# Fewer divided matrix products, at other places, in a tuned hybrid-attention layer; three small steps of the order moved

## The chip, the cores and the metric

One core of a Trainium2 chip runs the whole layer. The metric is device time in microseconds (us) of one execution, the median over runs. Each engine of the core (TensorE = PE, VectorE = DVE, ScalarE = ACT, GpSimd = POOL, SyncE = SP) works through its own list of instructions in order; they meet at semaphores.

## The reference, cut to what matters

```python
h = x                                              # 256 tokens x 2048
n = rmsnorm(h, g_mix);  z = n @ w_in               # 2048 x 5120
q, k, v, u = split(z)
a = moba_attention(q, k, v, bias)                  # 8 heads of 128; one block of 256 keys, so causal
c = conformer_conv(u)                              # gate, 31 taps per channel, layernorm, silu
h = h + concat(a, c) @ w_out                       # 2048 x 2048
h = h + cross_attention(rmsnorm(h), rmsnorm(mem))  # 4 heads, 256 memory tokens; wq, wk, wv, wo
h = h + square(relu(rmsnorm(h) @ w1)) @ w2         # 2048 x 8192 x 2048
return rmsnorm(h, g_final)
```

All in float32. About 200 MB of weights are read once.

## The kernel before, in words

The weights are cut into 200 chunks of 128 x 2048 numbers, one for each **step** of the program: 0 to 15 the conv projection (U), 16 to 23 V, 24 to 39 Q and K, 40 to 47 keys and values of the memory, 48 to 63 w_out, 64 to 67 wq, 68 to 71 wo, and from 72 four times 16 steps of w1 and 16 of w2 (w1 at 72, 104, 136 and 168).

Float32 accuracy comes from three products of rounded parts: a chunk is loaded (`raw`), ACT rounds it (`wh`), DVE takes the rest (`wl`, in six of the early steps POOL does), and the activations are split in the same way. `weight_stationary` (U, QK, w_out, wq, w1) issues, for each of 16 pairs of a 128-row piece i and a 128-column piece m of the chunk, `wh` x high, `wh` x low, `wl` x high, each over 256 tokens: 48 **products** in a step, numbered 0 to 47, and four units of 12. `act_stationary` (V, memory values, w2) keeps the activations still and moves 512 columns; there are 24 of these in a step.

The table `PARTED` (L43) names products which are **divided**: L342 to L344 issue the product as one matmul over 64 tokens and one over 192, with the weights loaded for both. Before, 8 steps had three divided products each.

The order is written by hand. The loop at L1007 goes through the steps and calls hooks: "early", "pre" and "late" ahead of a step's products, "mid" ahead of a unit (the number behind it), "post" behind the last. Within it ACT splits the chunk two steps ahead (`split_high`), DVE or POOL too (`split_low`), and `fill` puts as many of the 248 convolution taps between as DVE should have room for, by a cost model.

- `WARM` (L45): so many transposes of constants run on PE ahead of the first product.
- `spread_m` (L449 to L451): two transposes spread the memory's rmsnorm factor `r_m` over 128 partitions, ahead of unit 2 of step 16. `r_m` comes from `st_m.chain` (ahead of unit 2 of step 15), seven small DVE instructions and an ACT square root.
- `self_attention(b)` (L481), for two heads each, b = 0 to 3, s0 = 28 + 4b: `scores` behind step s0, softmax in s0 + 1, `transposes` of the probabilities ahead of unit 2 of s0 + 2 (then two ACT copies), `values` ahead of unit 2 of s0 + 3, `evac_o` at the start of s0 + 4. All of them take turns on two PSUM banks called `sm`.
- Cross attention, head h: `cx_q` (a DVE copy of the query), `cx_s` (scores on PE, maximum on DVE, exponentials on ACT, scaling on DVE), `cx_t` (transposes on PE, a copy on ACT), `cx_v` (values on PE). In step 66, ahead of unit 2, stood `cx_t(0)` and then `cx_s(1)`; `cx_v(0)` stands behind the step. At that step's start `wo_split0` (L747) splits a chunk of wo, two instructions on ACT and two on DVE.

Of the kernel before, what the change touches and what calls it, by code (L numbers as in the profile page):

```python
# [30 lines left out]
U0, V0, QK0, MK0, MV0, WOUT0, WQ0, WO0, MLP0, NSTEP = 0, 16, 24, 40, 44, 48, 64, 68, 72, 200  # L31
# [7 lines left out]
WOUT_ORDER = [(0, 0), (1, 0), (2, 0), (0, 1), (1, 1), (2, 1), (3, 0), (3, 1)]  # L39
STEP_US = 5.25  # L40


PARTED = {2: (3, 7, 11), 6: (24, 28, 32), 24: (3, 7, 11), 50: (3, 7, 11), 77: (24, 28, 32),  # L43
          104: (3, 7, 11), 136: (3, 7, 11), 168: (3, 7, 11)}
WARM = 14  # L45

ROOM = 128
ACT_SHIFT = (0, 0, 96, 96)
# [34 lines left out]
def tile_hybrid_block(ctx: ExitStack, tc: tile.TileContext, xT, memT, w, par, rel, gfin, out):  # L83
# [12 lines left out]
    def ring(shape=(P, 512)):  # L96
        return sb.tile(list(shape), F32, tag="ring", name=nm("ring"), bufs=7)

    def small():
        return sb.tile([P, 16], F32, tag="small", name=nm("small"), bufs=4)  # L100

    def bank(tag):
        return Bank(ps.tile([P, 512], F32, tag=tag, name=nm(tag), bufs={"mm": 4, "cv": 2, "sm": 2}[tag]))

    def mm(bk, o, lhsT, rhs, stop):
        pe.matmul(o, lhsT=lhsT, rhs=rhs, start=not bk.begun, stop=stop, skip_group_check=True)  # L106
        bk.begun = True
# [40 lines left out]
    warm = bank("sm")  # L148
    for i in range(WARM):
        pe.transpose(warm.ap[:, (i % 4) * P:(i % 4 + 1) * P], ones, ident)  # L150
# [4 lines left out]
    def at(place, j, fn, frac=0):  # L155
        hooks.setdefault((place, j), []).append((frac, fn))
# [97 lines left out]
    def spread(r):  # L254
        bk = bank("sm")
        for t in range(2):
            pe.transpose(bk.ap[:, t * P:(t + 1) * P], r[:, t:t + 1].to_broadcast([P, P]), ident)
        rb = sb.tile([P, T], F32, tag="Rb", name=nm("Rb"), bufs=2)
        act.copy(rb, bk.ap[:, :T])
        return rb  # L260
# [4 lines left out]
    def pair(ap):  # L265
        return ap.rearrange("p (a b) -> p a b", a=2)
# [33 lines left out]
    def weight_stationary(j, banks, kg, acts, kts=4, cols=512, last=None):  # L300
        units = []
        nf = cols // P
        for i in range(kts):
            def unit(i=i):
                for m in range(nf):
# [5 lines left out]
                    for n, (a, b) in enumerate(((h, hi), (h, lo), (l, hi))):  # L311
                        stop = last and i == kts - 1 and n == 2
                        if 3 * (nf * i + m) + n in PARTED.get(j, ()):
                            mm(bk, o[:, 0:64], a, b[:, 0:64], False)
# [19 lines left out]
    def block(j0, n, kind, acts, evac, place="pre", lag=0, tag="mm"):  # L334
        banks = []

        def open_banks():
            banks.extend([bank(tag), bank(tag)])

        for k in range(n):  # L340
            def make(k=k):
                if k == 0:  # L342
                    open_banks()
                return kind(j0 + k, banks, k, acts, last=(k == n - 1))  # L344
            pe_units[j0 + k] = make
        at(place, j0 + n + lag, lambda: evac(banks))
# [101 lines left out]

    def spread_m():  # L449
        RB["m"] = spread(r_m)  # L450
    at("mid", 16, spread_m, 2)  # L451
    for g in range(4):
        at("pre", (38, 39, 40, 42)[g], lambda g=g: split_act_group(g, memraw[g], G_MEM))

# [15 lines left out]
    def mix_tiles(key):  # L470
        if key not in mix:
            mix[key] = shifted(f"mix{key}", (S_SHIFT[key] + MIX_STEP) % ROOM)
        return mix[key]

    def evac_split(dst, i, src):
        hi, lo = dst
        act.activation(hi[:, i, :], src, AF.Copy)
        dve.tensor_sub(lo[:, i, :], src, hi.bitcast(F32)[:, i, :])

    def self_attention(b):  # L480
        st = {}  # L481
        s0 = QK0 + 4 * b + 4
        heads = (2 * b, 2 * b + 1)

        def evac_qk(banks):
            for h, bk in zip(heads, banks):
                st["qk", h] = ring((P, 2, T))
                dve.tensor_tensor(st["qk", h], pair(bk.ap), RB["qk"], op=OP.mult)

        def scores():  # L490
            for h in heads:
                bk = bank("sm")
                q, k = st["qk", h][:, 0, :], st["qk", h][:, 1, :]
                mm(bk, bk.ap[:, 0:P], q[:, 0:P], k[:, 0:P], True)
                mm(bk, bk.ap[:, P:3 * P], q[:, P:T], k, True)
                st["s", h] = bk.ap

        def softmax_a():
            for h in heads:
                pr, s = ring(), small()  # L500
                st["p", h], st["z", h] = pr, s
                for t, (lo, hi), bs in ((0, (0, P), bias[:, h, P:T]), (1, (P, 3 * P), bias[:, h, :])):
                    dve.tensor_tensor_reduce(pr[:, lo:hi], in0=st["s", h][:, lo:hi], in1=bs, scale=1.0,
                                             scalar=MASK, op0=OP.add, op1=OP.max, accum_out=s[:, t:t + 1])
                dve.tensor_scalar(s[:, 2:4], s[:, 0:2], -1.0, None, op0=OP.mult)

        def softmax_b():
            for h in heads:
                pr, s = st["p", h], st["z", h]
                for t, (lo, hi) in ((0, (0, P)), (1, (P, 3 * P))):  # L510
                    act.activation(pr[:, lo:hi], pr[:, lo:hi], AF.Exp, bias=s[:, 2 + t:3 + t],
                                   accum_out=s[:, 4 + t:5 + t])

        def softmax_c():
            for h in heads:
                pr, s = st["p", h], st["z", h]
                dve.reciprocal(s[:, 6:8], s[:, 4:6])
                for t, (lo, hi) in ((0, (0, P)), (1, (P, 3 * P))):
                    act.activation(pr[:, lo:hi], pr[:, lo:hi], AF.Copy, scale=s[:, 6 + t:7 + t])

        def transposes():
            for h in heads:
                bk = bank("sm")
                for i in range(3):
                    pe.transpose(bk.ap[:, i * P:(i + 1) * P], st["p", h][:, i * P:(i + 1) * P], ident)  # L525
                st["t", h] = ring()
                act.copy(st["t", h][:, 0:3 * P], bk.ap[:, 0:3 * P])

        def values():
            for h in heads:  # L530
                bk = bank("sm")
                c = slice(h * P, (h + 1) * P)
                mm(bk, bk.ap[:, 0:T], vv[0][:, 0, c], st["t", h][:, 0:T], False)
                mm(bk, bk.ap[:, P:T], vv[0][:, 1, c], st["t", h][:, T:3 * P], True)
                st["o", h] = bk.ap[:, 0:T]

        def evac_o():
            for h in heads:
                evac_split(mix_tiles(MIX[h // 4]), h % 4, st["o", h])

        block(QK0 + 4 * b, 4, weight_stationary, act_pair, evac_qk, place="early")
        at("post", s0, scores)
        at("pre", s0 + 1, softmax_a)
        at("late", s0 + 1, softmax_b)
        at("late", s0 + 1, softmax_c)
        at("mid", s0 + 2, transposes, 2)
        at("mid", s0 + 3, values, 2)
        at("pre", s0 + 4, evac_o)

    for b in range(4):  # L550
# [124 lines left out]
    def wq_units(h):  # L675
        def make():
            bk = cx["bank", h] = bank("cv")
            o = bk.ap[:, 0:T]
            j = WQ0 + h

            def unit(g):
                def go():
                    for i in range(4):
                        kt = 4 * g + i
                        s = slice(kt * P, (kt + 1) * P)
                        mm3(bk, o, (wh[j][:, s], wl[j][:, s]), act_pair(kt), kt == KT - 1)
                return go
            return [unit(g) for g in range(4)]
        return make

    def cx_q(h):
        cx["q", h] = ring()
        dve.tensor_copy(cx["q", h][:, 0:T], cx["bank", h].ap[:, 0:T])
# [17 lines left out]
    def cx_t(h):  # L711
        bk = bank("sm")
        for m in range(2):
            for t in range(2):
                pe.transpose(bk.ap[:, m * T + t * P:m * T + (t + 1) * P], cx["p", h][:, t, m * P:(m + 1) * P], ident)  # L715
        cx["t", h] = ring((P, 2, T))
        act.copy(cx["t", h], pair(bk.ap))

    def cx_v(h):
        bk = bank("sm")  # L720
        for m in range(2):
            mm(bk, bk.ap[:, 0:T], kv[1][:, m, h * P:(h + 1) * P], cx["t", h][:, m, :], m == 1)
        cx["o", h] = bk.ap[:, 0:T]

    def cx_e(h):
        if not cx_o:
            mix.clear()
            cx_o.append(mix_tiles("a0"))
        evac_split(cx_o[0], h, cx["o", h])

    for h in range(N_CROSS):
        pe_units[WQ0 + h] = wq_units(h)
        at("early", WQ0 + h + 1, lambda h=h: cx_q(h))
        if h < 3:
            at("mid", WQ0 + h + 1, lambda h=h: cx_s(h), 3 if h == 0 else 2)
        if h < 2:
            at("mid", WQ0 + h + 2, lambda h=h: cx_t(h), 2)
            at("post", WQ0 + h + 2, lambda h=h: cx_v(h))
            at("early", WQ0 + h + 3, lambda h=h: cx_e(h))

# [338 lines left out]
```

## Time and profile before

| | us |
|---|---|
| three runs, median (lowest to highest) | 1159.45 (1157.51 to 1162.56) |
| the profiled execution, its own time | 1160.12 |
| its span, first to last instruction | 1158.3 |
| PE busy | 1144.4 of the span |
| DVE, ACT, POOL busy | 705.5, 540.3, 123.2 |

PE's matmuls are pipelined: a busy PE is not one at its peak. How fast it goes is read from how many matmuls start in a stretch, or from the distance of their starts. The granted TensorE clock was 0.997 of full speed over the span.

### The profile page before, as it was taken

To read this page: it belongs to the slowest core of one execution; us is meant where nothing else is said; L and a number is where in the kernel's file an instruction comes from. 1 tells how busy PE (TensorE), PEld (TensorE's weight loads), DVE (VectorE), ACT (ScalarE), POOL (GpSimd) and SP (SyncE) were. 2 spreads that over 40 slices of the span, in tenths; PEclk is the share of its full clock that TensorE was granted. 3 is DMA by queue.
4 is the path that set the end of the run, shared out by engine and by line. 5 is a ranking of instruction groups with operands and counts; after the bars stand their busy time and mean duration, and the time that the engine had idled before them with its cause. 6 is when DMAs were issued, how large, how long until landed. Compare 5 with 4: busy or idle time off the path is not lost.

```text
span 1158.3 us, 18581 instructions
## 1 busy us (share of the span) xinstructions
PE 1144.4 (99%) x8038; PEld 1069.5 (92%) x8038; DVE 705.5 (61%) x821; ACT 540.3 (47%) x565; POOL 123.2 (11%) x104
## 2 busy tenths in 40 slices
PE   8999999999999999999999999999999999999997
PEld 8998899998999999998889998889999889999886
DVE  6699997878666768545444454554545554455443
ACT  7654335474655556444333444333454333444342
POOL 2282022102004003000000200000000000000112
PEclk9999999999999999999999999999999999999999
DMA  9874744455455535455555645555544555554541
GB/s 349 287 219 170 272 184 173 154 182 182 169 190 192 179 134 194 155 227 192 191 182 182 218 158 211 208 187 184 184 178 185 215 184 195 193 190 149 218 145 73
DMA packets 35289, 221.04 MB, mean 191 GB/s; under 512 B 3848, under 2 KB 7304, under 8 KB 9736
## 3 DMA queue, kind: packets, MB, share of 16 engines
q1 hardware_dynamic: 33024, 216.98, 51.7%
q10 hardware_dynamic: 2184, 2.88, 1.2%
q8 instruction: 63, 1.03, 0.4%
q14 instruction: 18, 0.15, 0.0%
HBM read 216.18 MB, written 3.67 MB: 190 GB/s over the span
## 4 chain that ended last, share of the span: by engine, by line
PE 92%; DVE 4%; ACT 1%; DMA 1%; issue 1%; ACTq 0%; POOL 0%; DVEq 0%
PE mm L106 86%; PE cv L106 3%; DVE cv L72 2%; DVE wl L72 2%; PE sm L106 2%; DMA raw<-in_w_dram 1%; ACT wh L172 0%; DMA hT<-in_xT_dram 0%; PE sm L840 0%; PE sm L525 0%; DVE small L72 0%; PE sm L715 0%; DVE ring L72 0%; ACT act L200 0%; POOL hp L420 0%
## 5 line engine op out<-in xcount | busy, mean ns | idle before, releaser
L72 DVE TENSOR_TENSOR wl<-raw,wh 128x2048 fp32r<-128x2048 f32 (+1 forms) x205 | 444.5, 2175 | 296.8 <-ACT wh L172 291.8
L172 ACT ACTIVATE wh<-raw 128x2048 fp32r<-128x2048 f32 x195 | 373.7, 1916 | 501.8 <-PE mm L106 448.2
L106 PE MATMUL mm<-act,wh 128*128 128x256 f32 (+1 forms) x3214 | 566.0, 280 | 1.3 <-ACT wh L358 1.3
L106 PEld LDWEIGHTS mm<-act,wh 128*128 128x128 f32 x3214 | 490.0, 188 | 2.2 <-ACT wh L358 1.6
L106 PE MATMUL mm<-act,wl 128*128 128x256 f32 x1607 | 447.0, 279 | 0.4 <-DVE wl L72 0.4
L106 PE MATMUL mm<-wh,s 128*128 128x512 f32 (+1 forms) x1040 | 319.1, 387 | 0.0
L106 PEld LDWEIGHTS mm<-act,wl 128*128 128x128 f32 x1607 | 301.2, 188 | 1.0 <-DVE wl L72 1.0
L106 PEld LDWEIGHTS mm<-wh,s 128*128 128x128 f32 x1040 | 194.3, 188 | 39.2
L106 PE MATMUL mm<-wl,s 128*128 128x512 f32 (+1 forms) x520 | 200.7, 386 | 0.0
L106 PEld LDWEIGHTS mm<-wl,s 128*128 128x128 f32 x520 | 97.7, 188 | 19.4
L72 DVE SCALAR_TENSOR_TENSOR cv<-hp,part,cv 128x256 f32<-128x256 f32 x240 | 97.6, 478 | 0.0
L72 DVE TENSOR_TENSOR s<-ring,s 128x512 fp32r<-128x512 f32 x32 | 22.2, 692 | 66.6 <-ACT s L828 66.6
L944 POOL TENSOR_TENSOR acc<-acc,gb 128x512 f32<-128x512 f32 x6 | 11.9, 2010 | 458.1 <-ACT ring L860 458.1
L106 PE MATMUL mm<-wh,act 128*128 128x512 f32 x192 | 60.1, 391 | 0.0
L225 POOL TENSOR_TENSOR acc<-acc,ring 128x512 f32<-128x512 f32 x17 | 39.9, 2344 | 147.0 <-ACT ring L224 146.3
L106 PE MATMUL mm<-mixa,wh 128*128 128x256 f32 (+1 forms) x258 | 45.6, 280 | 0.0
L106 PEld LDWEIGHTS mm<-wh,act 128*128 128x128 f32 x192 | 36.0, 188 | 7.4
L182 POOL TENSOR_TENSOR wl<-raw,wh 128x512 fp32r<-128x512 f32 x24 | 32.5, 1386 | 95.4 <-ACT wh L172 95.4
L106 PEld LDWEIGHTS mm<-mixa,wh 128*128 128x128 f32 x258 | 39.3, 188 | 0.2
L106 PE MATMUL mm<-wl,act 128*128 128x512 f32 x96 | 37.4, 389 | 0.0
L106 PE MATMUL mm<-mixa,wl 128*128 128x256 f32 (+1 forms) x129 | 35.7, 278 | 0.0
L106 PE MATMUL mm<-mixc,wh 128*128 128x256 f32 x192 | 32.7, 276 | 0.0
(141 smaller groups left out, 745.2 us busy)
## 6 DMA issues: line engine op xcount, KB each, us to landing
raw<-in_w_dram SPq DMA_DIRECT2D x199, 1024.0 KB, 4.8
mem<-in_memT_dram SPq DMA_DIRECT2D x4, 512.0 KB, 8.4
hT<-in_xT_dram SPq DMA_DIRECT2D x3, 512.0 KB, 8.5
dram_rev<-rev ACTq DMA_DIRECT2D x1, 1532.0 KB
raw<-in_w_dram SPq DMA_DIRECT2D x4, 256.0 KB, 5.7
bias<-dram_rev SPq DMA_DIRECT2D x1, 1024.0 KB, 8.2
gb<-in_gfin_dram SPq DMA_DIRECT2D x4, 256.0 KB, 7.4
out_dram<-acc SPq DMA_DIRECT2D x4, 256.0 KB, 2.7
```

The source lines that it names most:

```text
L72: return op(out, *args, **kw)
L106: pe.matmul(o, lhsT=lhsT, rhs=rhs, start=not bk.begun, stop=stop, skip_group_check=True)
L172: act.activation(wh[j], raw[j], AF.Copy)
L182: pool.tensor_sub(wl[j][:, s], raw[j][:, s], wh[j].bitcast(F32)[:, s])
L225: eng.tensor_tensor(self.acc, self.acc, sq, op=OP.add)
L944: pool.tensor_mul(d, d, gb[cb])
```

## The change

Twenty-four divided products become thirteen. The steps 2 and 72 have three (72 had none), the steps 6, 24, 50, 77, 104, 136 and 168 have one; in 6, 50 and 77 the one that stays was the first of the three. `WARM` goes from 14 to 27. `spread_m` goes from step 16 to step 18, its chain stays. The attention's `transposes` go one step later, into the step of its `values`, which go from the middle of that step to its end. `cx_t(0)` goes one unit later, so that `cx_s(1)` now stands ahead of it.

```diff
-PARTED = {2: (3, 7, 11), 6: (24, 28, 32), 24: (3, 7, 11), 50: (3, 7, 11), 77: (24, 28, 32),
-          104: (3, 7, 11), 136: (3, 7, 11), 168: (3, 7, 11)}
-WARM = 14
+PARTED = {2: (5, 20, 36), 6: (24,), 24: (5,), 50: (3,), 72: (6, 21, 37), 77: (24,), 104: (6,), 136: (6,), 168: (6,)}
+WARM = 27
@@ spread_m
-    at("mid", 16, spread_m, 2)
+    at("mid", 18, spread_m, 2)
@@ self_attention
-        at("mid", s0 + 2, transposes, 2)
-        at("mid", s0 + 3, values, 2)
+        at("mid", s0 + 3, transposes, 2)
+        at("post", s0 + 3, values)
@@ cross attention, h < 2
-            at("mid", WQ0 + h + 2, lambda h=h: cx_t(h), 2)
+            at("mid", WQ0 + h + 2, lambda h=h: cx_t(h), 3 if h == 0 else 2)
```

The start of step 104 on PE; `s` is the activation of w2, `act` that of w1, `mm` the PSUM bank. Before:

```order
L106 MATMUL mm_6238<-wh_6265,s_254_5813 128x512
L106 MATMUL mm_6373<-act_213_4730,wh_6301 128x256 x2
L106 MATMUL mm_6373<-act_213_4730,wl_6302 128x256
L106 MATMUL mm_6373<-act_213_4730,wh_6301 128x64
L106 MATMUL mm_6373<-act_213_4730,wh_6301 128x192
L106 MATMUL mm_6373<-act_213_4730,wh_6301 128x256
L106 MATMUL mm_6373<-act_213_4730,wl_6302 128x256
L106 MATMUL mm_6374<-act_213_4730,wh_6301 128x256
L106 MATMUL mm_6374<-act_213_4730,wh_6301 128x64
L106 MATMUL mm_6374<-act_213_4730,wh_6301 128x192
```

Now, with the line numbers two lower:

```order
L104 MATMUL mm_6246<-wh_6273,s_254_5821 128x512
L104 MATMUL mm_6381<-act_213_4737,wh_6309 128x256 x2
L104 MATMUL mm_6381<-act_213_4737,wl_6310 128x256
L104 MATMUL mm_6381<-act_213_4737,wh_6309 128x256 x2
L104 MATMUL mm_6381<-act_213_4737,wl_6310 128x256
L104 MATMUL mm_6382<-act_213_4737,wh_6309 128x64
L104 MATMUL mm_6382<-act_213_4737,wh_6309 128x192
L104 MATMUL mm_6382<-act_213_4737,wh_6309 128x256
L104 MATMUL mm_6382<-act_213_4737,wl_6310 128x256
```

Products 3, 7 and 11 were divided; product 6 is now, three products further from the 512-column work, and 3, 7 and 11 are whole.

The second place is ACT in step 66; `wo` is the split of wo, `ring ... small` with two inputs of `sm` the exponentials of a `cx_s`, the COPY that of a `cx_t`, `mixa` the output of a `cx_v`. Before:

```order
L705 ACTIVATE ring_4363,small_4362<-sm_4359,small_4362,rr 128x256 x2
L752 ACTIVATE wo_179_4387<-raw_4247 128x1024
L752 ACTIVATE wo_180_4388<-raw_4247 128x1024
L717 COPY ring_4423<-sm_4418 128x512
L705 ACTIVATE ring_4429,small_4428<-sm_4425,small_4428,rr 128x256 x2
L477 ACTIVATE mixa_188_4464<-sm_4461 128x256
```

Now:

```order
L703 ACTIVATE ring_4370,small_4369<-sm_4366,small_4369,rr 128x256 x2
L750 ACTIVATE wo_179_4394<-raw_4254 128x1024
L750 ACTIVATE wo_180_4395<-raw_4254 128x1024
L703 ACTIVATE ring_4429,small_4428<-sm_4425,small_4428,rr 128x256 x2
L715 COPY ring_4454<-sm_4449 128x512
L475 ACTIVATE mixa_188_4471<-sm_4468 128x256
```

The copy of head 0's transposes, which `cx_v(0)` reads, has moved behind the exponentials of head 1.

## Rows read from the trace of the kernel before

**Rows 1.** The page, busy time of each engine (share of the span, instructions)

```profile
PE 1144.4 (99%) x8038; PEld 1069.5 (92%) x8038; DVE 705.5 (61%) x821; ACT 540.3 (47%) x565; POOL 123.2 (11%) x104
```

**Rows 2.** Waits of PE: engine line waited for: us in total, times, longest

```profile
PE sm L257 <- DVE rr L72: 1.9, 1, 1.9
```

**Rows 3.** Windows, L106: from:to, us, PE busy (matmuls), weight loads, clock, DMA

```profile
48.00:95.00 47.00, 47.00 (x417) 47.00 (x416) 1.00 0.71 208
470.00:524.00 54.00, 54.00 (x479) 54.00 (x478) 1.00 0.52 196
618.00:706.00 88.00, 88.00 (x750) 88.00 (x749) 1.00 0.55 197
```

**Rows 4.** Timeline of PE, start of step 104: start, us, operation, shape of first, count

```profile
615.91 0.40 PE L106 MATMUL mm<-act,wh 128*128 128x256 f32 x2
616.15 0.28 PE L106 MATMUL mm<-act,wl 128*128 128x256 f32 x1
616.27 0.50 PE L106 MATMUL mm<-act,wh 128*128 128x64 f32 x3
616.61 0.28 PE L106 MATMUL mm<-act,wl 128*128 128x256 f32 x1
```

**Rows 5.** Windows, L106: steps 34 to 35, 35 to 36, 71 to 76

```profile
209.80:215.20 5.40, 5.40 (x48) 5.40 (x47) 1.00 0.50 194
216.80:224.60 7.80, 7.80 (x71) 7.80 (x70) 1.00 0.38 137
430.10:461.10 31.00, 31.00 (x265) 31.00 (x265) 1.00 0.54 186
```

**Rows 6.** Timeline of PE in step 77, first divided product

```profile
467.46 0.50 PE L106 MATMUL mm<-act,wh 128*128 128x64 f32 x3
467.80 0.28 PE L106 MATMUL mm<-act,wl 128*128 128x256 f32 x1
```

**Rows 7.** Timeline of PE in step 16, around `spread_m` (idle before, releaser)

```profile
101.63 0.39 PE L106 MATMUL mm<-wh,act 128*128 128x512 f32 x1
103.90 0.43 PE L257 MATMUL sm<-ident,rr 128*128 128x128 f32 x2 [1.88 <-DVE rr L72]
```

**Rows 8.** Window over steps 17 to 28, DVE alone: us, DVE busy (instructions), clock

```profile
107.10:169.50 62.40, 62.25 (x110) 1.00 0.57 210
```

**Rows 9.** Timeline of POOL, the third and fourth quarter of step 25's `wl`

```profile
149.33 3.36 POOL L182 TENSOR_TENSOR wl<-raw,wh 128x512 fp32r<-128x512 f32 x1
...
152.65 1.30 POOL L182 TENSOR_TENSOR wl<-raw,wh 128x512 fp32r<-128x512 f32 x1
```

**Rows 10.** Timeline of PE, start of step 24

```profile
144.99 0.40 PE L106 MATMUL mm<-act,wh 128*128 128x256 f32 x2
```

**Rows 11.** Timeline of PE in step 66: `cx_t(0)`, `cx_s(1)`, `cx_v(0)`

```profile
395.95 0.28 PE L106 MATMUL cv<-act,wl 128*128 128x256 f32 x1
396.69 0.72 PE L715 MATMUL sm<-ident,ring 128*128 128x128 f32 x4 [0.47 <-DVE ring L72]
397.28 1.10 PE L106 MATMUL sm<-kvt,ring 128*128 128x256 f32 x4
...
401.05 1.02 PE L106 MATMUL sm<-ring,kvt 128*128 128x256 f32 x4
```

**Rows 12.** Timeline of DVE there: `cx_q(1)`, the maximum for head 1

```profile
396.72 0.42 DVE L72 COPY ring<-cv 128x256 f32<-128x256 f32 x1
...
399.32 0.68 DVE L72 TENSOR_REDUCE small<-sm 128x2 f32<-128x512 f32 x1
```

**Rows 13.** Timeline of ACT there: copy of `cx_t(0)`, end of head 1's exponentials

```profile
397.75 0.57 ACT L717 COPY ring<-sm 128x512 f32<-128x512 f32 x1
...
400.87 0.56 ACT L705 ACTIVATE ring<-sm,small,rr 128x256 f32<-128x256 f32 x1
```

**Rows 14.** Windows, all engines: us, then PE, PEld, DVE, ACT, POOL; clock

```profile
7.86:11.26 3.40, 3.40 (x16) 3.12 (x15) 3.00 (x6) 2.59 (x6) 0.00 (x0) 0.50 1.03 398
```

**Rows 15.** Timeline of ACT, the first quarter of step 1's `wh`

```profile
13.15 0.63 ACT L358 ACTIVATE wh<-raw 128x512 fp32r<-128x512 f32 x1 [2.18 <-DMA raw<-in_w_dram]
```

## The prediction

> **What bounds the kernel now.** I read the page's busy times first: PE is busy 1144.4 of 1158.3 us [rows 1]. The waits of PE come next: the largest behind the start is one of 1.9 us for DVE, at `spread_m` [rows 2]. So hardly any time is to be had from waiting; what counts is how fast PE goes while it works. For that I counted matmuls in windows that hold only 256-column products, taking off the two that are in flight at the left edge. In 48 to 95 (steps 6 to 15) there are 417, in 470 to 524 (steps 78 to 87) 479: 47.00/415 and 54.00/477, 0.1132 us each, the **fast pace**. In 618 to 706 (steps 104 to 119) there are 750: 88.00/748 = 0.1176, the **slow pace** [rows 3]. The clock is 1.00 in both, the upper level of 2.4 GHz. The instructions are the same ones on the same tiles, and nothing is waited for. The difference, 0.0044 to 0.0046 (I take 0.0045), holds for hundreds of products in a row.
>
> What separates the stretches is how they began. Step 77 had its first divided product twelve products after the transposes that spread a factor, and the fast pace follows directly. Step 6 does the same, also twelve products after its own, and step 50 after 27. In steps 24, 104, 136 and 168 the first divided product is the fourth after 512-column work [rows 4], and behind all three divided ones the slow pace stays: 104's row shows it, 136's and 168's show x749 in as many us. Small matmuls put between products can switch the pace too: after the attention's `transposes` it is slow (48 records in 5.40 us), after most `values` fast (71 in 7.80) [rows 5]. So the two paces are two ways in which the row of products can run, and a divided product can move it from slow to fast, at some places.
>
> **The long w1 stretches, 104, 136, 168.** Each is 768 products from 615.91 on; before, 768 x 0.1177 and three divisions are 90.7 us. A division's own cost: product 3 of step 104, in two parts, and the whole one behind it take 616.27 to 616.61 = 0.34 us where two slow products take 0.235, so 0.105; at the fast pace 467.46 to 467.80, again 0.34, against 0.226: 0.114 [rows 4, 6]. Now product 6 is divided alone. If it switches the pace: six slow products 0.71, the division 0.34 for two, 760 x 0.1132 = 86.0; together 87.1, a gain of 3.6 each, 10.8 for three. If it doesn't, two divisions fewer give 0.21 each, 0.6 in all. I take the first: product 6 has the place that worked in steps 6, 50 and 77, the first of its triple (`wh` x high), and stands three whole products further from the 512-column work, where the row has had time to settle. No row shows a division at product 6, so the other end stays in the range.
>
> Does the faster row find its chunks? In steps 78 to 87 the same loop ran at the fast pace for ten steps with no PE wait.
>
> **The short stretches.** Step 72 (new, three tries): 263 products, 430.1 to 461.1, ran slow [rows 5]; three divisions cost 0.32, some 252 fast products give 1.13: gain 0.8. Step 2: three before and three now; about 169 products up to the next interruption, 0.76. Steps 6, 50, 77: two divisions fewer each, at the fast pace, 6 x 0.114 = 0.7; the one that switched stays. Step 24: two fewer, 0.2, and if product 5 switches, 233 products of steps 24 to 28 give 1.05. Bounds for all of it: 3.5 if each switches, about 0.8 if only the old ones do.
>
> **`spread_m`.** Before, PE stood from 101.63 + 0.23 to 103.90: 2.04 us [rows 7]. Two steps later r_m is long there, so this wait goes. What is late next: DVE and POOL follow the convolution taps here, DVE busy for 62.25 of the 62.40 us from 107.1 to 169.5 [rows 8], and don't come earlier when PE does. The nearest of their results is `wl` of step 25, which POOL makes in four quarters; the third took 3.36 us in place of 1.30 and ended at 152.69, the fourth at 153.95 [rows 9]. Step 25 began at 144.99 + 48 x 0.1177 + 3 x 0.105 = 150.95 [rows 10], and its product 26, the first to read the third quarter, stood at 154.0: 1.3 us to spare. PE now comes earlier against POOL by 2.04 + 0.2 (step 24's divisions) + 70 x 0.0045 = 2.55. So **a new wait of about 1.25 us** in step 25 takes over, and `spread_m` nets 0.8 (0 to 2.0). The restart may also set the row back to the slow pace for the 166 products up to the next interruption: 0 to 0.75, I take 0.4. POOL's queue holds only the fourth quarter behind it, due at 154.1, just in time.
>
> **Attention.** Four times, 24 products fewer run between `transposes` and `values`, at the slow pace: 4 x 24 x 0.0045 = 0.4. The two ACT copies between them had 48 products as cover and have 24, 2.8 us; ACT's list holds nothing new ahead of them, and before, PE never waited for them. What hides them is those 24 products; without them PE would stand until the second copy is done. `values` fills the two `sm` banks that `scores` of the next heads needs 48 products later, 5.4 us for `evac_o` to empty them. I take no wait.
>
> **`cx_t(0)`.** It waited for DVE's scaling of head 0 (due at 395.95 + 0.12, start 396.69, 0.6), and this wait goes. But `cx_s(1)`, now first, needs `cx_q(1)`, a DVE copy that ends at 397.14 [rows 11, 12]: it waits from 396.07 to 397.2, 1.1 us where 0.6 was waited. Twelve products and the transposes then bring PE to 399.9, twelve more to 401.3, where `cx_v(0)` needs the ACT copy. This now stands behind head 1's exponentials, which end at 401.43 whatever PE does, since DVE takes the maximum only at 399.32, behind its two wo instructions [rows 12, 13]. The copy takes 0.57: 402.0, so `cx_v(0)` starts at 402.05, not 401.05. The step ends **1.0 us later**. Bounds: a gain of 0.8 (both waits hidden) to this loss. I take the loss, since each of its times is a row.
>
> **Constants in front.** Thirteen more transposes fill PE's gap ahead of its first product. Before, the clock fell to 0.50 (1.2 GHz) from 7.86 to 11.26, behind that gap [rows 14]. Even so PE had to wait for step 1's first chunk, which landed at 13.15 [rows 15]: what is won ahead of that is waited there. I take 0; if the clock fell later, 16 products in 3.40 us for 29 would cost 1.5.
>
> **The sum**, against the profiled execution's 1160.12 (the median of the runs is 0.7 lower, within their spread of 5): 10.8 + 0.8 + 0.76 + 0.7 + 0.2 + 1.05 - 0.4 + 0.8 + 0.4 - 1.0 = 14.1. 1160.1 - 14.1 = **1146**.
>
> **Rivals.** *The new places don't switch the long rows.* For it: no division behind 512-column work has switched yet, in four stretches with three tries each; against it: all these were the first twelve products. Then 10.8 becomes 0.6: 1156; with step 2, 24 and 72 failing too, 1158. [...]
>
> *Some of the three long ones switch*: 1149.5 to 1153.5.
>
> *Slower: the single tries fail where threes worked*, in steps 6, 50 and 77. Each place is the same product, but what runs ahead of it has changed. Some 420, 700 and 490 products would fall back to slow, 1610 x 0.0045 = 7.2. With the long rows staying slow too, 1158 + 7.2 = 1165 to 1166. It decides the sign as soon as the loss passes the 10.8 of the long rows less the rest, so it needs both failures.
>
> *The change doesn't do what it says*: `spread_m`'s gain is given to step 25 as above, 1 us either way, within each case.
>
> **How the numbers follow.** Forecast (1142 to 1149.5) 0.68; some of three 0.08; no switch in the long rows 0.17; slower 0.04; the rest is spread. 0.5% is 5.8 us, about what a measurement of this kernel can tell from no change: faster is below 1153.7, which the first two cases are: 0.76. Same 0.19, slower 0.05. The range reaches from 1142 (`spread_m` whole, `cx_t` without loss, all short rows fast) to 1157, into the no-switch case, and leaves out under 2 in 10.
>
> **What would show it.** Right: the windows of steps 105 to 119 and their like hold a matmul each 0.113 us; PE's only large new waits are for POOL's `wl` near 150 and for an ACT copy near 400; none for `rr` at step 18. Wrong: the long rows at 0.1176, or steps 7 to 15, 51 to 63 or 78 to 87 no longer at 0.1132.

## The result, and the profile after

The changed kernel takes **1145.93 us** in the median of four runs (1145.53 to 1146.86); the kernel before, beside it, 1160.03 (1157.51 to 1162.56). The ratio is 0.9883, with a 95% interval from 0.9864 to 0.9902: 1.2% faster, where 1146 was forecast. The profiled execution took 1145.53, its span is 1143.7. Line numbers are two lower than before (L106 is now L104).

The page's busy times, to be held against [rows 1]: PE still fills its span and lost 14.4 us of busy time, with two instructions more.

```profile
PE 1130.0 (99%) x8040; PEld 1055.2 (92%) x8040; DVE 705.2 (62%) x821; ACT 540.3 (47%) x565; POOL 123.0 (11%) x104
```

Windows that hold only 256-column products, PE alone (from:to, us, PE busy (matmuls), clock, DMA share, GB/s), to be held against [rows 3]. They lie in steps 6 to 15, 78 to 86, and in the three long w1 stretches from 104, 136 and 168:

```profile
48.00:94.00 46.00, 46.00 (x409) 1.00 0.72 213
472.00:517.00 45.00, 45.00 (x400) 1.00 0.53 196
614.00:699.00 85.00, 85.00 (x752) 1.00 0.56 204
788.00:873.00 85.00, 85.00 (x752) 1.00 0.53 194
963.00:1047.00 84.00, 84.00 (x743) 1.00 0.52 192
```

With two off for those in flight, the last three rows give 85.00/750, 85.00/750 and 84.00/741, all 0.1133 us a product: the fast pace of the first two rows, where the kernel before had 0.1176. The clock is at its upper level, 2.4 GHz, in all of them, as before.

The timeline of PE at the start of step 104 (start, us, operation, shape of the first, count), to be held against [rows 4]. The row with 128x64 is the divided product 6 and the product behind it:

```profile
612.05 0.40 PE L104 MATMUL mm<-act,wh 128*128 128x256 f32 x2
...
612.76 0.50 PE L104 MATMUL mm<-act,wh 128*128 128x64 f32 x3
613.10 0.28 PE L104 MATMUL mm<-act,wl 128*128 128x256 f32 x1
613.21 0.39 PE L104 MATMUL mm<-act,wh 128*128 128x256 f32 x2
```

Six slow products take 0.71, the division 0.34, and from 613.10 the row is fast.

The waits of PE (engine, line, waited for: us in total, times, longest) no longer have the row of `rr` [rows 2], and have three new ones:

```profile
PE mm L104 <- POOL wl L180: 1.2, 1, 1.2
PE sm L104 <- DVE ring L70: 1.0, 1, 1.0
...
PE sm L104 <- ACT ring L715: 0.5, 1, 0.5
```

They stand in step 25 and twice in step 66, as these rows of PE's timeline show. The first is `spread_m` at its new place, with nothing waited for (against [rows 7]); then the product of step 25 that waits for the third quarter of `wl`; then `cx_s(1)` and `cx_v(0)` (against [rows 11]):

```profile
111.82 0.38 PE L255 MATMUL sm<-ident,rr 128*128 128x128 f32 x2
...
151.86 0.38 PE L104 MATMUL mm<-act,wl 128*128 128x256 f32 x1 [1.21 <-POOL wl L180]
...
393.04 1.13 PE L104 MATMUL sm<-kvt,ring 128*128 128x256 f32 x4 [0.96 <-DVE ring L70]
...
397.90 1.13 PE L104 MATMUL sm<-ring,kvt 128*128 128x256 f32 x4 [0.51 <-ACT ring L715]
```

Starts of the same PE instructions in both profiled executions give the account by place. "So far" is before less after, the next column what the part ahead of that place gained, the last the prediction's terms for it. The times are rounded, so a difference is good to about 0.02.

| PE reaches | before | after | so far | part | predicted |
|---|---|---|---|---|---|
| the first division of step 6 | 46.52 | 45.83 | 0.69 | 0.69 | 0 (front) + 0.76 (step 2) |
| step 24 | 144.99 | 141.97 | 3.02 | 2.33 | 0.23 (step 6) + 2.04 (`spread_m`) |
| the first attention scores | 173.57 | 170.79 | 2.78 | -0.24 | 0.2 + 1.05 - 0.4 (step 24) - 1.25 (new wait) |
| the sums behind the attention | 283.43 | 279.50 | 3.93 | 1.15 | 0.4 |
| the last product ahead of the first wait in step 66 | 395.95 | 391.80 | 4.15 | 0.22 | 0.23 (step 50) |
| the transposes for cross-attention head 1 | 404.74 | 401.69 | 3.05 | -1.10 | -1.0 |
| the sums behind the row of steps 71 to 76 | 461.14 | 457.51 | 3.63 | 0.58 | 0.8 (step 72) |
| step 104 | 615.91 | 612.05 | 3.86 | 0.23 | 0.23 (step 77) |
| step 136 | 793.75 | 786.30 | 7.45 | 3.59 | 3.6 |
| step 168 | 971.59 | 960.54 | 11.05 | 3.60 | 3.6 |
| the last step's 256-column matmuls | 1143.99 | 1129.35 | 14.64 | 3.59 | 3.6 |

### The profile page after: what moved, and what is told of

It reads as the page before. It is cut to its first block, busy times and chain, and to the rows that moved or that the text cites. A ratio compares the mean times of both kernels' runs of the same rounds, so it can differ in the third digit from the quotient of the medians.

```text
span 1143.7 us, 18577 instructions
## 1 busy us (share of the span) xinstructions
PE 1130.0 (99%) x8040; PEld 1055.2 (92%) x8040; DVE 705.2 (62%) x821; ACT 540.3 (47%) x565; POOL 123.0 (11%) x104
## 4 chain that ended last, share of the span: by engine, by line
PE 92%; DVE 4%; ACT 1%; DMA 1%; POOL 1%; issue 0%; ACTq 0%; POOLq 0%
PE mm L104 87%; PE cv L104 3%; DVE cv L70 2%; DVE wl L70 2%; PE sm L104 2%; DMA raw<-in_w_dram 1%; POOL wl L180 1%; DMA hT<-in_xT_dram 0%; ACT wh L170 0%; PE sm L838 0%; DVE small L70 0%; PE sm L523 0%; DVE wo L70 0%; ACT ring L703 0%; ACT act L198 0%
## 5 line engine op out<-in xcount | busy, mean ns | idle before, releaser
L104 PE MATMUL mm<-act,wh 128*128 128x256 f32 x3209 | 550.0, 277 | 0.7 <-ACT wh L356 0.7
L104 PEld LDWEIGHTS mm<-act,wh 128*128 128x128 f32 x3209 | 483.8, 188 | 1.6 <-ACT wh L356 1.1
L104 PE MATMUL mm<-act,wl 128*128 128x256 f32 (+1 forms) x1603 | 442.6, 276 | 1.7 <-POOL wl L180 1.2
L104 PE MATMUL mm<-wh,s 128*128 128x512 f32 (+1 forms) x1040 | 319.1, 387 | 0.0
L104 PEld LDWEIGHTS mm<-act,wl 128*128 128x128 f32 x1603 | 300.7, 188 | 2.3 <-POOL wl L180 1.4
L104 PEld LDWEIGHTS mm<-wh,s 128*128 128x128 f32 x1040 | 194.3, 188 | 39.3
L104 PE MATMUL mm<-wl,s 128*128 128x512 f32 (+1 forms) x520 | 200.7, 386 | 0.0
L104 PEld LDWEIGHTS mm<-wl,s 128*128 128x128 f32 x520 | 97.7, 188 | 19.3
L104 PE MATMUL mm<-wh,act 128*128 128x512 f32 x192 | 60.2, 391 | 0.0
L104 PE MATMUL mm<-mixa,wh 128*128 128x256 f32 x257 | 45.4, 280 | 0.0
L104 PEld LDWEIGHTS mm<-wh,act 128*128 128x128 f32 x192 | 36.0, 188 | 7.5
L104 PEld LDWEIGHTS mm<-mixa,wh 128*128 128x128 f32 x257 | 39.2, 188 | 0.2
L104 PE MATMUL mm<-wl,act 128*128 128x512 f32 x96 | 37.4, 389 | 0.0
L104 PE MATMUL mm<-mixa,wl 128*128 128x256 f32 x128 | 35.5, 278 | 0.0
L104 PE MATMUL mm<-mixc,wh 128*128 128x256 f32 x192 | 32.7, 276 | 0.0
```

## The experiments

Theory: a division moves a row of products from the slow pace to the fast one if it stands at the right place in the row; `spread_m`, the new wait in step 25 and `cx_t(0)` act as the prediction reckoned. Rivals are in the expectations. Edits are against the changed kernel unless said otherwise. Each kernel was timed with the kernel before beside it, and that one's median lay between 1157.27 and 1160.03; so medians of two experiments can differ by 2 us for that alone, and the ratios and the starts in the traces decide.

**The long rows alone**, and **all but the long rows**.

```diff
 (the kernel before)
-          104: (3, 7, 11), 136: (3, 7, 11), 168: (3, 7, 11)}
+          104: (6,), 136: (6,), 168: (6,)}
```

> The kernel before with one edit: steps 104, 136 and 168 divide product 6 alone; all else as before. Theory (a division at product 6 moves the row from the slow pace to the fast one): 87.1 us in place of 90.7 for each 768 products, 10.8 us in all, so 1149 and windows of steps 105 to 119 at 0.113 us a product. Rival (the earlier start of PE in the changed kernel, not the place, made the long rows fast): the rows stay at 0.1176, two divisions fewer give 0.2 each, 1159.

```diff
-... 77: (24,), 104: (6,), 136: (6,), 168: (6,)}
+... 77: (24,)}
```

> The changed kernel without any division in steps 104, 136 and 168. Theory: the three long rows stay slow from their first product on, 760 x 0.0045 = 3.4 more each, less three divisions of 0.11: 1145.9 + 10 = 1156. Rival (the long rows come in fast by themselves, since something ahead of them changed): 1145.6, three divisions fewer.

Measured: 1149.54 (1146.97 to 1150.27; ratio to before 0.9913, 0.9894 to 0.9933) and 1156.29 (1154.12 to 1157.12; ratio 0.9977, 0.9968 to 0.9987). A window inside step 104's stretch, first of the one, then of the other:

```profile
616.00:700.00 84.00, 84.00 (x743) 1.00 0.57 205
```

```profile
617.00:702.00 85.00, 85.00 (x725) 1.00 0.55 198
```

84.00/741 = 0.1134 against 85.00/723 = 0.1176; the other two stretches read alike. Ten of the fourteen us hang on three instructions, and neither an earlier start nor anything else in the change is needed for it.

**Other products in the long rows.**

```diff
-104: (6,), 136: (6,), 168: (6,)
+104: (3,), 136: (7,), 168: (8,)
```

> The changed kernel with product 3 divided in step 104, product 7 in step 136, product 8 in step 168, in place of 6. Theory A (one of three: in a given row only products of one place in their triple can switch it, here the first, and only when the row has settled behind the 512-column work): all three rows stay slow, 1145.9 + 3 x 3.4 = 1156. Theory B (distance alone: any product from 6 on switches): step 104 stays slow, 136 and 168 are fast, 1149.4. Theory C (a single division switches and threes in a row do not): all three fast, 1146.

Measured: 1156.24, one run. Windows in the three stretches:

```profile
614.00:699.00 85.00, 85.00 (x724) 1.00 0.56 199
792.00:877.00 85.00, 85.00 (x724) 1.00 0.52 188
970.00:1055.00 85.00, 85.00 (x724) 1.00 0.52 188
```

All slow: distance alone (theory B) and "a single one" (C) fall.

```diff
-104: (6,), 136: (6,), 168: (6,)
+104: (9,), 136: (25,), 168: (384,)
```

> The changed kernel with product 9 divided in step 104 (first of its triple), product 25 in step 136 (second of its triple), product 384 in step 168 (first of its triple, half way through the row). Theory A (one of three): 104 fast from product 9, 136 slow throughout, 168 slow for 384 products and fast for 384: + 0.0 + 3.4 + 1.7, 1151. Theory B (distance alone): 104 and 136 fast, 168 as above: 1147.7. A theory by which only the first dozen products can switch a row: 104 fast, 136 and 168 slow: 1152.8.

The third part of this edit did nothing: a step has only 48 products, so no 384 exists, and stretch 168 ran undivided; what was expected of it falls away. Measured: 1153.85, one run. The windows:

```profile
617.00:700.00 83.00, 83.00 (x735) 1.00 0.56 203
793.00:878.00 85.00, 85.00 (x725) 1.00 0.52 186
968.00:1053.00 85.00, 85.00 (x724) 1.00 0.51 189
```

Product 9 switches its row, 25 does not: A. By the starts of steps 136, 168 and the last step the two slow rows cost 6.7; 0.75 of the rest is step 2's row, which ran slow here (below).

**A second try behind a failed one.**

```diff
-104: (6,), 136: (6,), 168: (6,)
+104: (7, 18), 136: (8, 18), 168: (3, 18)
```

> The changed kernel with two divisions in each long row: products 7 and 18 in step 104, 8 and 18 in step 136, 3 and 18 in step 168. The first of each failed where it stood alone. Theory A (the place in the triple decides, and a try that fails changes nothing for a later one some products on): all three rows turn fast at product 18, each 12 slow products and one division dearer than in the changed kernel, 3 x 0.16: 1146.4. Rival (a try that fails leaves a row that later tries don't switch, as the threes of the kernel before would suggest): all three slow, 1156.

Measured: 1145.99, one run. Windows behind product 18:

```profile
616.00:699.00 83.00, 83.00 (x735) 1.00 0.57 203
790.00:873.00 83.00, 83.00 (x735) 1.00 0.52 191
965.00:1048.00 83.00, 83.00 (x734) 1.00 0.53 191
```

All fast: a failed try spoils nothing ten products on. But then product 11 in step 24 should have worked before, being the third of its triple as the 5 that works there now. The starts in the traces, which resolve 1 ns, show why it did not. In a slow row the three intervals of a triple are not equal. In the undivided row of step 104 (all but the long rows) the first 30 products are followed by the next on average 117.7 ns after the first of a triple, 117.5 after the second and 118.5 after the third. Behind the three divisions of the kernel before (products 15 to 44) it is 118.6, 117.4, 117.6: the long interval has moved to the first. Hence a finer theory, that the divided product must be the one next behind the long interval:

```diff
-104: (6,), 136: (6,), 168: (6,)
+104: (3, 7, 11, 24), 136: (3, 7, 11, 25),
+168: (3, 7, 11, 26)
```

> The changed kernel with the three divisions of before (products 3, 7, 11) in each long row and a fourth some way behind: product 24 in step 104 (first of its triple), 25 in step 136 (second), 26 in step 168 (third). Theory A, made finer from the starts in the traces so far: in a slow row one of the three intervals of a triple is about 1 ns longer than the other two, and a division switches the row where the divided product is the one next behind it. In a row without divisions the longest follows the third product, so the first one switches; behind the three divisions of the kernel before it follows the first, so now the second should: step 136 turns fast at product 25, 104 and 168 stay slow, 1145.9 + 3.7 + 3.7 + 0.5 = 1153.8. Rival 1 (the place stays the first of the triple): step 104 fast, 136 and 168 slow, the same time with another row fast. Rival 2 (three divisions so close leave a row that nothing switches): all slow, 1157.

Measured: 1154.43, one run. Windows behind the fourth division:

```profile
620.00:702.00 82.00, 82.00 (x699) 1.00 0.56 202
795.00:877.00 82.00, 82.00 (x726) 1.00 0.52 193
970.00:1052.00 82.00, 82.00 (x699) 1.00 0.50 184
```

82.00/724 = 0.1133 in step 136's stretch alone, 82.00/697 = 0.1176 in the others: the row that was named, and the place that failed in the experiment with 25 above. In all thirteen traces 86 divided products stand at least six products into a slow row, with no other division within nine products; many are the same place in another trace. All 86 did what this theory says: 68 switched, 18 did not. Eleven more, product 5 of step 24, have only five products ahead of them; all switched, but in six of them two of the three intervals are equal, so that the theory can't be read there. Too near the start it fails: product 3 of a long row stands behind an interval of 120 ns, the longest so far, and in none of eight rows did it switch. And a division in a row that was already fast never set it back, in 58 cases. What makes the two paces and the long interval is not shown by any run.

**`spread_m` back at step 16.**

```diff
-    at("mid", 18, spread_m, 2)
+    at("mid", 16, spread_m, 2)
```

> The changed kernel with spread_m back at step 16. The prediction's account: the wait of 2.0 us near 100 returns, and the wait for POOL's wl in step 25 (1.2 to 1.7 us in the runs so far) goes, since PE comes to it 2 us later; net 0.5 to 0.8 slower, 1146.5, and steps 25 to 28 then run at the pace that step 24's division sets. Rival (the move is worth its whole wait, and step 25's wait is there either way): 2.0 slower, 1148.

Measured: 1146.57 (1146.32 to 1147.27; ratio 0.9896, 0.988 to 0.9913). PE's timeline there:

```profile
103.29 0.43 PE L255 MATMUL sm<-ident,rr 128*128 128x128 f32 x2 [2.01 <-DVE rr L70]
```

The wait is back, and the one for POOL is gone from the list of waits. The move trades 2.0 for the 1.2, as reckoned; the medians' 0.6 is within the runs' spread.

**POOL's queue.** What holds step 25's `wl` back was only bounded in the prediction. POOL's timeline in the changed kernel:

```profile
144.71 1.31 POOL L401 TENSOR_TENSOR csum<-hp,hp 128x512 f32<-128x512 f32 x1 [32.63 <-DVE cv L70]
145.98 7.08 POOL L180 TENSOR_TENSOR wl<-raw,wh 128x512 fp32r<-128x512 f32 x4
```

ACT had finished the `wh` that this `wl` needs at 138.65. POOL takes its list in order, and ahead of the four quarters stood a sum that waited for DVE's convolution taps.

```diff
             if i == 1:
-                csum[0] = sb.tile([P, 2, T], F32, tag="acc512", name="csum")
-                pool.tensor_add(csum[0], hp[0][:, :, CONV_K - 1:], done)
+                def first_sum():
+                    csum[0] = sb.tile([P, 2, T], F32, tag="acc512", name="csum")
+                    pool.tensor_add(csum[0], hp[0][:, :, CONV_K - 1:], done)
+                at("late", 23, first_sum)
```

> The changed kernel with POOL's first sum over the convolution's outputs (csum, step 23) put behind the four quarters of step 25's wl in POOL's queue. Account tested: wl of step 25 is late not because POOL is slow but because the sum ahead of it in POOL's queue waits for DVE's taps until 144.7, while its high part was there at 138.7. Then the four quarters end near 144, step 25's wait (1.5 in the changed kernel) goes, and steps 25 to 28 keep the pace that step 24's division gave: 1144.4. Rival (POOL is slow in this stretch whatever its order, as the quarter of 3.4 us suggests): the wait stays or moves to step 26, 1145.9.

Measured: 1144.20 (1142.81 to 1144.39; ratio 0.9874, 0.9859 to 0.9888).

```profile
139.47 5.78 POOL L180 TENSOR_TENSOR wl<-raw,wh 128x512 fp32r<-128x512 f32 x4 [26.81 <-ACT wh L170]
145.29 1.31 POOL L402 TENSOR_TENSOR csum<-hp,hp 128x512 f32<-128x512 f32 x1
```

The quarters now end at 145.25, no product of step 25 waits, and nothing new is late: the order is enough. Between the starts of step 24 and of the scores, 1.48 us more are gained than in the changed kernel. The rival is half right, though: in the changed kernel the third quarter took 3.3 us and the others 1.3, and with 1.3 it would have ended at 149.8, ahead of the product that waits (due at 150.5), in the old order too. The timelines of DVE and POOL there show why it was slow:

```profile
148.13 2.56 DVE L70 TENSOR_TENSOR wl<-raw,wh 128x2048 fp32r<-128x2048 f32 x1
148.50 3.31 POOL L180 TENSOR_TENSOR wl<-raw,wh 128x512 fp32r<-128x512 f32 x1
```

It starts while DVE subtracts a `wl` of its own, and ends 1.12 behind DVE's end at 150.69. Of the 312 quarters in the thirteen traces, 13 start inside such a subtraction of DVE: in all eleven traces with the old order it is this third one, in the two with the new order the first (2.00 here). Each ends 1.12 to 1.17 behind DVE's end; the other 299 take 1.28 to 1.33 us. So POOL's quarter stood until DVE was done. The wait in step 25 needed both, the sum ahead in POOL's list and DVE's subtraction over the third quarter.

**`cx_t(0)` back at unit 2.**

```diff
-            at("mid", WQ0 + h + 2, lambda h=h: cx_t(h), 3 if h == 0 else 2)
+            at("mid", WQ0 + h + 2, lambda h=h: cx_t(h), 2)
```

> The changed kernel with cx_t(0) back at unit 2. The prediction's account (its move lost 1.0 us): one wait of 0.7 near 396 in place of 1.24 and 0.78, and a time of 1144.9, below the changed kernel. Rival (the two waits only move time that PE would have waited for DVE or ACT a little later): a new wait of about as much in steps 67 to 70, 1145.9.

Measured: 1143.95 (1143.66 to 1146.89; ratio 0.988, 0.9864 to 0.9896). PE's timeline, `cx_t(0)` and the transposes for the next head:

```profile
393.00 0.72 PE L713 MATMUL sm<-ident,ring 128*128 128x128 f32 x4 [0.46 <-DVE ring L70]
...
401.05 0.60 PE L713 MATMUL sm<-ident,ring 128*128 128x128 f32 x4
```

From the product ahead of the first wait (392.27) to those transposes it takes 8.78, in the changed kernel 9.89: 1.1 won back, and no wait took its place. The medians, 2.0 apart, don't measure it: the ratios, 0.988 and 0.9883, can't be told apart.

**Attention and the constants in front undone.**

```diff
-        at("mid", s0 + 3, transposes, 2)
-        at("post", s0 + 3, values)
+        at("mid", s0 + 2, transposes, 2)
+        at("mid", s0 + 3, values, 2)
```

```diff
-WARM = 27
+WARM = 14
```

> The changed kernel with the attention's transposes and values at their places of before and 14 constant transposes in front. The prediction's account: attention costs 0.4 more over four blocks, the front nothing: the clock falls behind the gap near 7 as before, and PE still waits for the first chunk to about 14.6; 1146.3. Rival for the attention (the gap between the two decides only which products are slow): no change, 1145.9. Rival for the front (the fall of the clock sets PE back): 1.5 more, 1147.8.

Measured: 1147.35 (1145.65 to 1148.05; ratio 0.9901, 0.9887 to 0.9916); the total mixes both with rows of chance, so the places decide. From scores to scores the second and third pair of heads take 25.26 and 25.26, in the changed kernel 25.15 and 25.15: 0.1 a pair, so 0.4 for four, as predicted. (The first pair hangs on its row's pace, see below.) In front, things did not go as expected: the first products ran at half pace to 10.6 (last section), PE went through step 1 without the wait at 14, and it reached product 5 of step 2 at 20.38, against 20.75 in the changed kernel: nothing is won there by more constants.

**The mendings together**: POOL's sum behind `wl` and `cx_t(0)` back, as above, and

```diff
-PARTED = {2: (5, 20, 36), ...
+PARTED = {2: (5, 19, 36), ...
```

> The changed kernel with the three mendings together: POOL's first sum behind step 25's wl, cx_t(0) back at unit 2, and step 2's three divisions at products 5, 19 and 36, one of each place in the triple (in the changed kernel 5 and 20 have the same place). If the parts add up: the changed kernel's 1145.9 less 1.5 to 1.7 less 1.1, and step 2's row of products fast at the latest from product 36 on: 1143, below every kernel so far. Rival (what is won at these places is waited for further on): 1144 as the better of the parts alone.

Measured: **1142.51** (1141.86 to 1145.41; ratio to before 0.9862, 0.9841 to 0.9883), the lowest median and ratio here. Over the changed kernel (ratio 0.9883, 0.9864 to 0.9902) the times alone don't show a gain, since the intervals overlap; the starts do: 1.48 between step 24 and the scores, 1.11 in step 66. Of the waits of PE behind the start, these are left:

```profile
PE mm L104 <- ACT wh L356: 0.7, 2, 0.4
PE sm L715 <- DVE ring L70: 0.5, 1, 0.5
PE mm L104 <- DVE wl L70: 0.4, 2, 0.2
```

Step 2's row turned fast at product 5 in the profiled execution, so its second and third place were not put to the test.

**Rows of chance.** Rows that begin behind a wait (the first two columns) or behind the small matmuls of cross-attention (the third) come in at either pace, or with the long interval at another place, from one execution to the next. Each trace is of another kernel, but nine of them run the same instructions up to the end of step 2, and in three of these nine its row stayed slow to product 36 or to its end. Products in the same windows of each profiled execution, those in flight at the left edge included (129 and 130 are slow, 134 and 135 fast):

| | 25.2:40.2, step 2's row | 154:169, steps 26 to 28 | 442:457, the row of steps 71 to 76 |
|---|---|---|---|
| before | 130 | 130 | 129 |
| after | 135 | 135 | 135 |
| the long rows alone (no division in 72) | 130 | 129 | 135 |
| all but the long rows | 135 | 130 | 134 |
| products 3, 7, 8 | 134 | 130 | 135 |
| products 9, 25 | 130 | 135 | 135 |
| second try | 135 | 129 | 135 |
| fourth try | 135 | 130 | 135 |
| `spread_m` back | 135 | 135 | 135 |
| `cx_t(0)` back | 135 | 129 | 134 |
| attention and front undone | 130 | 130 | 134 |
| POOL's sum later | 129 | 134 | 135 |
| the mendings together | 135 | 134 | 134 |

Step 2's tries 5 and 20 are both third of their triple and 36 is first. Where the starts asked for the second, in three traces, the row stayed slow throughout; where they asked for the first, in one, it turned at 36. Behind POOL's wait steps 26 to 28 were fast in two traces of eight (with attention and front undone it is only 0.14 us long); in the three with step 24's division and without that wait, in all.

## Why the prediction was right

**The long rows** (predicted 10.8, measured 3.59 + 3.60 + 3.59 = 10.78). Step by step as reckoned: six slow products, one division, 760 fast ones. Both reasons given for product 6 hold in these rows: first of its triple (7, 8 and 25 failed, 9 and 18 worked) and further behind the 512-column work (3 failed). But "first of its triple" is no rule for other rows: step 24 asked for the third, the row behind three divisions for the second. What decides, some products into the row, is where the long interval lies, which the prediction did not see; that its reason held in the long rows was in part luck.

**The front and step 2** (0.76, 0.69): right in this execution; step 2 began at 20.16, before at 20.08. In four of the nine others with the same three tries the row stayed slow to product 36 or to its end, so on average the term is worth less.

**`spread_m` and step 25** (2.04 less 1.25): the wait went whole, and the new one is 1.37 (starts at 150.38 and 151.86, less a product). POOL's third quarter did come earlier, by 0.88 (its end 151.81, before 152.69), about the 0.92 that PE had gained ahead of step 16 and that this working left out. The mechanism, POOL's quarters late against an earlier PE, is shown by taking it away: `spread_m` back removes the wait, and so does POOL's order. What the prediction did not see is that the lateness came with a place in POOL's list and with DVE's subtraction over the third quarter, and that moving one instruction in the list keeps the whole 2.0.

**Step 24** (0.2 + 1.05 - 0.4): that product 5 switches had no reason in the prediction, whose "first of its triple" spoke against it; it did in all eleven traces, as product 11 had not before, and that is luck. The fall back to the slow pace behind the new wait, for which 0.4 was set aside, did not come in this execution; in six of the seven others with that wait it did. So -0.24 stands against -0.40.

**Attention** (0.4, measured 1.15): mis-sized in this execution. The move itself is worth 0.4, as the run without it shows. The rest comes from the first pair of heads, whose row came in fast (steps 26 to 28, above): 25.05 from scores to scores against 25.89 before. Where it came in slow, with products 3, 7 and 8, the part took 109.35 against 109.85 before, 0.5.

**`cx_t(0)`** (-1.0, measured -1.10): right to the instruction. Taken with the 4.15 gained by then, the prediction's 397.2 and 402.05 for the two waits' ends are 393.05 and 397.90; the rows show 393.04 and 397.90. Both waits, for the copy of the query and for the ACT copy behind head 1's exponentials, are the named ones.

**Step 72** (0.8, measured 0.58): mis-sized. The prediction took 252 products behind the division as fast; but its window [rows 5] begins with step 71, product 6 of step 72 stands 54 products into it, and only 204 were. 48 x 0.0045 is the missing 0.2. And the slow pace of that row before was chance: in ten of the eleven other traces it was fast before any division. In nine of these the three tries only cost: the part is 1.20 to 1.25 with them, and 1.54 in the one without. The prediction's lower bound for the short rows, 0.8, leaves the 0.32 of failed tries out.

**Constants in front** (0): right. The bound of 1.5 was not touched.

So the total of 14.64 is 0.5 above the sum because of the attention's row (0.75) and step 24's (0.16), less what step 72 and a few hundredths elsewhere fell short. That the median came within 0.1 of 1146 is luck, since each row of chance moves an execution by some 0.6 to 0.8. Of the rivals none came; "the new places don't switch" is what the kernel without these divisions shows, at 1156.29, and "some of three" with one fast row ran at 1153.85 and 1154.43.

## What to carry to other kernels

Where one engine is busy all the time, compare the distance of its starts between stretches with the same instructions: four per cent of an instruction, held for thousands of them, was worth more here than all waits together. A single divided matmul can move such a row from one pace to the other, but only at a place that the row's own start decides; behind a wait that place is open, so spread the tries over all remainders and some ten products apart (a try costs 0.1 us and did no harm to a fast row), and measure more than one execution. When an engine is brought forward, look at what stands ahead of the late result in its maker's list, and at what DVE does while POOL works, before giving the time up: one instruction moved was worth the whole wait.

## What the runs showed of the hardware beyond that

- The two paces at one granted clock, 0.1133 and 0.1177 us for 256 columns, are stable for 768 products. In the fast row the starts are 113, 113 and 114 ns apart, in the undivided slow one of step 104 on average 117.4, 117.6 and 118.3; a division switches the slow one where it falls next behind the long interval. The long 512-column rows showed one pace, 226.7 ns, in both kernels. The Trainium skill, TensorE: Matmul & The Clock Gate, section Back-to-back issue gap, has a formula for the gap of an isolated matmul, from which I estimate 109.2 ns for 256 columns; for a stream of weight loads and matmuls, as here, it says that both set the spacing. No row of 256-column products here runs at 109.2.
- The row of the granted clock does not show everything at the start. In the run with 14 constant transposes PE stood from 4.7 to 6.1, and then the first products started 0.213 us apart up to 10.6, as at the lower of the two levels (256 columns at 1.2 GHz are 213 ns; in the kernel before, starts 0.213 apart from 9.15 on go with the 0.50 of [rows 14]), while the window reads 1.00:

```profile
7.23:10.44 3.21, 3.21 (x17) 1.00 1.03 403
```

  3.21/15 = 0.214. The trace has no record of the clock ahead of 10.81. With 27, PE worked on, the transposes went from 0.213 to 0.109 us apart at 5.8, and the first products came 0.118 apart. The Trainium skill, TensorE: Matmul & The Clock Gate, Part 1: The HAM clock gate, has the array begin throttled until work releases it; the starts agree, the window's column does not.
- PE gets no further by the longer run of constants. With 14 of them it comes to step 1 later and waits there for 0.4 us at most, with 27 earlier and waits for the first chunk. Step 2 begins at 19.79 to 20.08 in the three traces with 14, and at 19.85 to 20.34 in the ten with 27.
- A 128x512 subtraction of POOL that starts inside a 128x2048 one of DVE stands until that one is done: 13 of 13 ended 1.12 to 1.17 us behind it, where the 299 others took 1.28 to 1.33 in all.
